# Group-norm roots taken on columns, and low weight parts formed by adding transfers, in a hybrid decoder layer

## The chip, the cores and the metric

The kernel runs on one core of a Trainium2 chip, with five engines that work side by side: TensorE (PE, with its weight loads as PEld), VectorE (DVE), ScalarE (ACT), GpSimd (POOL) and SyncE (SP, which only issues transfers). Sixteen DMA engines move data for all issuers. The metric is the device time of one execution in microseconds (us). Durations of single instructions are given in us or ns as the trace has them.

## The reference

One layer of a decoder trunk on a sequence of 1024 tokens with 1024 channels, in float32. A normalised input `hn` is projected once, and the projection is cut into the inputs of three mixers and their gates; the three branches are projected, gated and summed, and an MLP follows:

```
proj = hn @ w_in                                   # 1024 x 10256
ya = gmlp_mixer(za);  yb = rg_lru_mixer(zb);  yc = ssd_mixer(zc, xbc, dt_raw)
merged = sum_k sigmoid(gate_k) * (y_k @ w_branch_k)
h = h + merged @ w_out
h = h + relu(rms_norm(h) @ w_mlp_up)**2 @ w_mlp_down
out = rms_norm(h)
```

The change touches the last step of the SSD mixer and the weights of `w_in` and `w_branch_k`. The SSD mixer has four groups of 256 channels. Its output `y`, multiplied by silu(z), is normalised within each group, token by token:

```
yg = y.reshape(bsz, seq, 4, 256)
yg = yg * lax.rsqrt(jnp.mean(yg * yg, axis=-1, keepdims=True) + EPS)
y  = yg.reshape(bsz, seq, 1024) * norm_g
```

So one root is wanted for each token and group, 4096 in all.

## The kernel before

**Tiles and split operands.** Activations lie with channels on the 128 partitions and tokens along the free axis, in two halves of 512 tokens. A product in float32 is made from three products of a rounded type: each operand is split into a high part (a rounded copy) and a low part (the operand less its high part), and high x high, high x low and low x high are added in PSUM. `split` (L128 to L133) makes the pair: L132 copies on ACT, L133 subtracts on DVE or POOL.

**Units.** Most of the input projection runs as units (`one_unit`, L558): one unit makes 128 output channels of 1024 tokens, 48 matmuls of 512 columns at L554, and hands the PSUM tile `ps` to a `post` function. There are two `ps` buffers, so a unit may start once the post two units back has read its own. Its weights come from `wtile` (L521 to L529): a transfer issued by SP brings a 512 KB tile `raw` (two buffers), and the split makes `wh` and `wl` in a pool of six, which are three pairs. `ahead` keeps the weights of the present unit and of two more in the making: the pair of unit n+2 takes the buffers of unit n-1. Of every three tiles, two are subtracted on DVE and one on POOL. There are 74 such tiles: 50 of `w_in` in the first stage of the run, and 24 of the three `w_branch` matrices later. In each unit the first four matmuls use `wh` alone, the fifth is the first that reads `wl`.

**Side work.** After each unit the waiting generators do one step. For each SSD group (`ssd_stages`) the steps are `rows_in`, `s1_`, `s2_`, `s3_` and `s4_` for either half of the tokens. `rows_in` and `s2_` issue broadcasts from the DRAM scratch `acs_d` on POOL's queue (L662 to tiles `e`, L701 to tiles `h`). `s3_` multiplies the decayed terms (L728, L732 on PE, L735 to L738 on DVE) and squares the result (L740 on ACT, L741 on POOL). `s4_` takes the roots: a matmul with a tile of ones (L746) puts the sum over 128 channels into every partition, and a square root on ACT (L748), a reciprocal (L749) and four more operations on DVE (L750 to L753) make a tile of 128 x 512 roots, each partition holding the same row; L756 scales `z`, and L757 stores it. LRU units (`lru_units`) end in matmuls at L812, tanh and exp on ACT, a root on ACT (L824), products on POOL (L823, L826), and a scan on DVE (L827). `conv` (L574 to L577) reads a `ps` tile once on ACT (L575) and three times on DVE (L577). The four PSUM tiles `aux` are shared by all side work.

**What sets the order.** In this stage a scheduler puts the instructions of each engine in order by its own estimate of their times; the engines then run their queues strictly in that order, and a transfer's issue waits in its engine's queue for its data. The later stages (`with tc.manual_schedule()`) run in program order.

Of the kernel before, what the change touches and what calls it, by code (L numbers as in the profile page):

```python
# [8 lines left out]
F32 = mybir.dt.float32  # L9
F32R = mybir.dt.float32r  # L10
I32 = mybir.dt.int32
AF = mybir.ActivationFunctionType
ALU = mybir.AluOpType
# [3 lines left out]
P = 128  # L17
# [5 lines left out]
EPS = 1e-6  # L23
# [13 lines left out]
def trunk_kernel(ctx: ExitStack, tc: tile.TileContext, x, norm_mix_g, w_in, b_gate, gmlp_ln_g, gmlp_ln_b,  # L37
# [4 lines left out]
    nc = tc.nc  # L42
    x, w_in, b_gate, out = x[0], w_in[0], b_gate[0], out[0]
    w_out, w_up, w_dn = w_out[0], w_mlp_up[0], w_mlp_down[0]

    base = ctx.enter_context(tc.tile_pool(name="base", bufs=1))
# [28 lines left out]
    def half_(shape=(P, HF), dt=F32):  # L75
        return halfp.tile(list(shape), dt, tag="half", name=nm("h"))

    def aux():
        return auxp.tile([P, HF], F32, tag="aux", name=nm("aux"))
# [6 lines left out]
    tt = nc.vector.tensor_tensor  # L86
    stt = nc.vector.scalar_tensor_tensor
    ts = nc.vector.tensor_scalar
    actv = nc.scalar.activation
    mm = nc.tensor.matmul  # L90
# [37 lines left out]
    def split(dst_hi, dst_lo, src, eng=None, cast=None):  # L128
        if cast:
            cast.tensor_copy(out=dst_hi, in_=src)  # L130
        else:
            actv(dst_hi, src, AF.Copy)  # L132
        (eng or nc.vector).tensor_tensor(out=dst_lo, in0=src, in1=dst_hi.bitcast(F32), op=ALU.subtract)  # L133
# [151 lines left out]
    with tc.manual_schedule():  # L285
# [19 lines left out]
        ident = base.tile([P, P], F32, name="ident")  # L305
# [4 lines left out]
        nc.gpsimd.affine_select(out=tri, in_=ones, pattern=[[1, P]], compare_op=ALU.is_ge, fill=0.0,  # L310
                                base=0, channel_multiplier=-1)
        g2c = base.tile([P, 2 * KD], F32, name="g2c")
        eps4 = base.tile([P, 1], F32, name="eps4")
        nc.vector.memset(eps4, 4.0 * EPS)
        ss, rs = sm(NCH, "ss"), sm(NCH, "rsx")
        v2[NCH - 1] = act()

# [70 lines left out]
        for c in range(1, NCH):  # L388
# [5 lines left out]
            sq = gelu_in(c - 1)  # L394
# [123 lines left out]
            self.op["A22"] = [[t[:, 4 * p + kk, :] for kk in range(4)] for p in range(2)]  # L518


    def wtile(src, n=[0]):  # L521
        raw = rawp.tile([P, KD, P], F32, tag="raw", name=nm("raw"))
        nc.sync.dma_start(out=raw, in_=src.rearrange("(k p) e -> p k e", p=P))
        hi = wp.tile([P, KD, P], F32R, tag="w", name=nm("wh"))
        lo = wp.tile([P, KD, P], F32R, tag="w", name=nm("wl"))
        n[0] += 1
        split(hi, lo, raw, nc.gpsimd if n[0] % 3 == 0 else nc.vector)
        return hi, lo

    queue, ready, pending = [], [], []  # L530
# [118 lines left out]
    def ssd_stages(g, S):  # L649
# [5 lines left out]
        def tok(c):  # L655
            return slice(c * P, (c + 1) * P)
# [40 lines left out]
        def s2_(half):  # L697
            for j in range(2):
                t = er[half, j] = half_((P, 4, P))
                for h in range(2):  # L700
                    nc.gpsimd.dma_start(out=t[64 * h:64 * h + 64], in_=acs_v[1, half * 4:half * 4 + 4, 4 * g + 2 * j + h, :].partition_broadcast(64))  # L701
            for q in (2 * half, 2 * half + 1):
                if q == 0:
                    pv[0] = half_((P, 2, 256))
                    nc.gpsimd.memset(pv[0][:, 0, :], 0.0)
                st = aux()
                for cc in range(2):
                    mm(st[:, cc * 256:cc * 256 + 256], Bt[:, 2 * q + cc, :], xw[q][:, cc].rearrange("p h d -> p (h d)"), start=True, stop=True)
                for cc in range(2):
                    c = 2 * q + cc  # L710
                    if c == NCH - 1:
                        continue
                    if cc == 1:
                        pv[q + 1] = half_((P, 2, 256))
                    dst = pv[(c + 1) // 2][:, (c + 1) % 2, :]
                    for h in range(4):
                        col = c * 16 + 4 * g + h
                        o = slice(h * 64, h * 64 + 64)
                        stt(out=dst[:, o], in0=pv[q][:, cc, o], scalar=etot[:, col:col + 1],
                            in1=st[:, cc * 256 + h * 64:cc * 256 + h * 64 + 64], op0=ALU.mult, op1=ALU.add)  # L720

        def s3_(half):
# [17 lines left out]
                actv(sq[half, j], Z[:, tk], AF.Square)  # L740
            nc.gpsimd.tensor_tensor(out=sq[half, 0], in0=sq[half, 0], in1=sq[half, 1], op=ALU.add)  # L741

        def s4_(half):
            tk = hsl(half)
            vs = aux()
            mm(vs, ones, sq[half, 0], start=True, stop=True)  # L746
            r, q = half_(), half_()
            actv(r, vs, AF.Sqrt, scale=1.0 / 256, bias=eps4)  # L748
            nc.vector.reciprocal(out=r, in_=r)  # L749
            tt(out=q, in0=r, in1=r, op=ALU.mult)  # L750
            stt(out=q, in0=vs, scalar=256 * 4.0 * EPS, in1=q, op0=ALU.add, op1=ALU.mult)
            ts(out=q, in0=q, scalar1=-0.5 / 256, scalar2=1.5, op0=ALU.mult, op1=ALU.add)
            tt(out=r, in0=r, in1=q, op=ALU.mult)  # L753
            for j in range(2):
                Z = S["z", j]
                stt(out=Z[:, tk], in0=Z[:, tk], scalar=va[:, SNG + 2 * g + j:SNG + 2 * g + j + 1], in1=r, op0=ALU.mult, op1=ALU.mult)  # L756
                nc.gpsimd.dma_start(out=yd["c"][2 * g + j][:, tk], in_=Z[:, tk])  # L757

        rows_in(0)
# [6 lines left out]
        rows_in(1)  # L766
        yield
        s1_(1)
        s4_(0)
        yield  # L770
        s2_(1)
        yield
        s3_(1)
        yield
        yield
        s4_(1)


# [846 lines left out]
```

## Time and profile before

Three runs of the kernel took 2033.77, 2035.14 and 2036.89 us; the median is 2035.14 us. The profiled execution is a separate one, and its own time is 2038.13 us.

| | value |
|---|---|
| median of three runs | 2035.14 us |
| profiled execution, its own time | 2038.13 us |
| its span, first to last instruction | 2036.3 us |
| PE busy | 1968.3 us (97%) |
| DVE busy | 1286.2 us (63%) |
| ACT busy | 875.0 us (43%) |
| POOL busy | 328.1 us (16%) |
| mean granted TensorE clock | 0.986 of full speed |

Busy time is time in which an instruction of the engine ran; issues of transfers and waits on semaphores are not in it. PE's matmuls are pipelined and their ends are modelled, so the cost of a matmul is best read from start to start. A wait is put down to the producer that came last. The first stage with units and side work lies between 127 and 800 us, the products of the gates between 800 and 1030 us, the 24 branch units between 1030 and 1290 us.

### The profile page before, as it was taken

Reading aid. Unit: us, or ns where it says so; the run is one execution under the profiler, and the core shown is the slowest. Engines: PE = TensorE matmul, PEld = TensorE weight load, DVE = VectorE, ACT = ScalarE, POOL = GpSimd, SP = SyncE. Lnnn points to the kernel's source line nnn. Section 1 sums busy time; section 2 is a strip of 40 time slices with the busy share of each in tenths; the row PEclk is TensorE's granted clock in tenths of the full one; section 3 lists DMA queues with packets and bytes.
Section 4 is the critical chain, followed back from the end, with each engine's and each line's share of the span. In section 5 each row is a group of like instructions: output and inputs, shape, how many; then the busy total and the mean of one; then the engine's idle time right before and its main releaser. Section 6 shows DMA issues by size and latency. Waiting matters only on the chain.

```text
span 2036.3 us, 23707 instructions
## 1 busy us (share of the span) xinstructions
PE 1968.3 (97%) x9168; PEld 1639.5 (81%) x9168; DVE 1286.2 (63%) x1835; ACT 875.0 (43%) x1302; POOL 328.1 (16%) x362
## 2 busy tenths in 40 slices
PE   8999999999999999999999999999899999999996
PEld 7998878777778788788888888887688887888885
DVE  5596786874877787544452324336766557787787
ACT  6423554554546533444451111246555555253243
POOL 4012132231231343000000230000111111000000
PEclk8999999999999999999999999999999999999998
DMA  4223235224242343333393332421444438644532
GB/s 156 76 104 79 64 77 115 62 63 88 63 96 65 73 144 119 120 107 111 114 320 121 117 94 93 165 83 54 163 134 161 160 129 301 216 131 144 184 107 92
DMA packets 204517, 247.77 MB, mean 122 GB/s; under 512 B 11396, under 2 KB 148820, under 8 KB 204404
## 3 DMA queue, kind: packets, MB, share of 16 engines
q1 hardware_dynamic: 175636, 144.91, 23.9%
q0 software_dynamic: 22832, 79.84, 12.4%
q10 hardware_dynamic: 5936, 21.51, 3.0%
q8 instruction: 72, 1.18, 0.2%
q14 instruction: 41, 0.34, 0.1%
HBM read 178.97 MB, written 67.24 MB: 121 GB/s over the span
## 4 chain that ended last, share of the span: by engine, by line
PE 77%; DVE 10%; ACT 5%; DMA 4%; issue 2%; POOL 2%; SPq 0%; DVEq 0%; ACTq 0%; POOLq 0%
PE ps L554 31%; PE aux L478 30%; PE gps L478 6%; PE aux L257 4%; PE aux L1155 2%; DVE a L827 1%; DVE a L577 1%; DMA h<-acs_d 1%; PE aux L812 1%; DMA lr<-in_lru_w_i_dram 1%; DMA a<-in_x_dram 1%; ACT a L1196 1%; PE aux L856 1%; DVE rsq_q L111 1%; ACT a L132 1%
## 5 line engine op out<-in xcount | busy, mean ns | idle before, releaser
L554 PE MATMUL ps<-xn,wh 128*128 128x512 f32 x1600 | 440.5, 396 | 12.2 <-DVE a L577 12.2
L554 PEld LDWEIGHTS ps<-xn,wh 128*128 128x128 f32 x1600 | 301.4, 190 | 78.6 <-issue 12.7
L554 PE MATMUL ps<-xn,wl 128*128 128x512 f32 x800 | 248.9, 392 | 0.0
L478 PE MATMUL aux<-a,b 128*128 128x512 f32 x864 | 197.3, 389 | 0.0
L478 PEld LDWEIGHTS aux<-a,b 128*128 128x128 f32 x864 | 162.2, 188 | 33.6
L132 ACT ACTIVATE wh<-raw 128x1024 fp32r<-128x1024 f32 x74 | 78.0, 1055 | 255.8 <-PE ps L554 221.1
L554 PEld LDWEIGHTS ps<-xn,wl 128*128 128x128 f32 x800 | 151.7, 190 | 32.0
L478 PE MATMUL aux<-b,wt 128*128 128x512 f32 x672 | 156.9, 389 | 0.0
L478 PEld LDWEIGHTS aux<-b,wt 128*128 128x128 f32 x672 | 126.2, 188 | 26.1
L478 PE MATMUL aux<-b,b 128*128 128x512 f32 x480 | 110.6, 389 | 0.0
L1050 DVE SCALAR_TENSOR_TENSOR a<-a,ps 128x1024 f32<-128x1024 f32 x22 | 26.8, 1220 | 131.2 <-PE ps L554 86.3
L1377 DVE TENSOR_TENSOR a<-aux,a 128x512 f32<-128x512 f32 x112 | 77.1, 689 | 50.4 <-PE aux L478 50.4
L133 POOL TENSOR_TENSOR wl<-raw,wh 128x1024 fp32r<-128x1024 f32 x24 | 60.9, 2539 | 293.8 <-ACT wh L132 293.7
L133 DVE TENSOR_TENSOR wt<-a,wt 128x1024 fp32r<-128x1024 f32 x50 | 61.3, 1226 | 70.8 <-ACT wt L132 70.8
L478 PEld LDWEIGHTS aux<-b,b 128*128 128x128 f32 x480 | 90.1, 188 | 18.7
L133 DVE TENSOR_TENSOR wl<-raw,wh 128x1024 fp32r<-128x1024 f32 x50 | 66.2, 1325 | 45.9 <-ACT wh L132 38.6
L133 DVE TENSOR_TENSOR a<-a,a 128x1024 fp32r<-128x1024 f32 (+1 forms) x64 | 63.8, 1004 | 49.3 <-ACT a L132 49.2
L132 ACT ACTIVATE b<-wt 128x1024 fp32r<-128x1024 f32 x60 | 61.8, 1053 | 69.4 <-DMA wt<-u_d 65.0
L554 PE MATMUL ps<-c,wh 128*128 128x512 f32 x320 | 85.5, 389 | 0.0
L478 PE MATMUL aux<-a,wt 128*128 128x512 f32 x336 | 80.3, 396 | 3.3 <-ACT a L1254 3.3
L132 ACT ACTIVATE a<-a 128x1024 fp32r<-128x1024 f32 (+1 forms) x64 | 55.0, 879 | 56.4 <-DVE a L1329 45.2
L478 PEld LDWEIGHTS aux<-a,wt 128*128 128x128 f32 x336 | 64.1, 191 | 17.6 <-ACT a L1254 4.2
(336 smaller groups left out, 3699.5 us busy)
## 6 DMA issues: line engine op xcount, KB each, us to landing
wt<-u_d SPq DMA_DIRECT2D x54, 512.0 KB
raw<-in_w_in_dram SPq DMA_DIRECT2D x50, 512.0 KB
u_d<-a POOLq DMA_DIRECT2D x48, 512.0 KB, 5.1
g_d<-a POOLq DMA_DIRECT2D x24, 512.0 KB, 2.9
a<-g_d ACTq DMA_DIRECT2D x22, 512.0 KB
rt<-in_w_mlp_up_dram SPq DMA_DIRECT2D x17, 512.0 KB
a<-acs_d POOLq DMA_DIRECT2D x32, 256.0 KB, 8.1
a<-in_w_mlp_down_dram SPq DMA_DIRECT2D x16, 512.0 KB
```

What stands on the lines that cost most here:

```text
L111: stt(out=q, in0=r, scalar=nh, in1=r, op0=ALU.mult, op1=ALU.mult)
L132: actv(dst_hi, src, AF.Copy)
L133: (eng or nc.vector).tensor_tensor(out=dst_lo, in0=src, in1=dst_hi.bitcast(F32), op=ALU.subtract)
L257: mm(ps[:, :nt], X.tok(a, k, c), wk[k][w], start=(k == 0 and i == 0), stop=(k == KD - 1 and i == 2))
L478: mm(ps, lhs[l][kk], rhs[r][kk], start=(new and n == 0), stop=(n == 11), skip_group_check=not new)
L554: mm(ps[:, hsl(h)], w[wi][:, k, :], a.rhs(ai, k, h), start=(n == 0), stop=(n == 3 * KD - 1))
L577: stt(out=dst[:, j:], in0=ps[:, :T - j], scalar=taps[3 - j], in1=dst[:, j:], op0=ALU.mult, op1=ALU.add)
L812: mm(ps, w[wi][:, q * P:(q + 1) * P], S["xs"][half][ai], start=(n == 0), stop=(n == 2))
L827: nc.vector.tensor_tensor_scan(out=y[:, tk], data0=m, data1=ti, initial=(0.0 if half == 0 else y[:, HF - 1:HF]), op0=ALU.mult, op1=ALU.add)
L1050: stt(out=t, in0=t, scalar=1.0, in1=ps, op0=ALU.add, op1=ALU.mult)
L1155: mm(ps, M.tok(a, k, c), wo[nb][k][w], start=(k == 0 and a + w == 0), stop=(k == KD - 1 and a == 1))
L1377: tt(out=h, in0=ps, in1=h, op=ALU.add)
```

## The change

In `wtile` the low part is no longer subtracted by DVE or POOL. ACT copies `raw` to `wh`, then copies `wh` with factor -1 to `wl`, and POOL issues a transfer from `raw` to `wl` that adds to what lies there. In the SSD, `s4_` is cut in two. `roots_` sums squares with `sq` as the stationary operand and one column of ones as the moving one, 128 tokens at a time, so that the sums of 512 tokens land as four columns of 128; `rsqrt_cols` (three operations on DVE and twelve on POOL, all on 128 x 4 elements) makes the roots, in a tile `groot`. `s4_`, one step later, spreads each column of roots over all partitions by a matmul with the column, repeated 128 times, as stationary operand and the identity as moving one; L756 then reads the roots from PSUM. `rsqrt_cols` was there before, for the norm of the input rows.

```diff
@@ -310,8 +310,7 @@
         nc.gpsimd.affine_select(out=tri, in_=ones, pattern=[[1, P]], compare_op=ALU.is_ge, fill=0.0,
                                 base=0, channel_multiplier=-1)
         g2c = base.tile([P, 2 * KD], F32, name="g2c")
-        eps4 = base.tile([P, 1], F32, name="eps4")
-        nc.vector.memset(eps4, 4.0 * EPS)
+        groot = base.tile([P, 8], F32, name="groot")
         ss, rs = sm(NCH, "ss"), sm(NCH, "rsx")
         v2[NCH - 1] = act()
 
@@ -518,13 +517,14 @@
             self.op["A22"] = [[t[:, 4 * p + kk, :] for kk in range(4)] for p in range(2)]
 
 
-    def wtile(src, n=[0]):
+    def wtile(src):
         raw = rawp.tile([P, KD, P], F32, tag="raw", name=nm("raw"))
         nc.sync.dma_start(out=raw, in_=src.rearrange("(k p) e -> p k e", p=P))
         hi = wp.tile([P, KD, P], F32R, tag="w", name=nm("wh"))
         lo = wp.tile([P, KD, P], F32R, tag="w", name=nm("wl"))
-        n[0] += 1
-        split(hi, lo, raw, nc.gpsimd if n[0] % 3 == 0 else nc.vector)
+        actv(hi, raw, AF.Copy)
+        actv(lo, hi.bitcast(F32), AF.Copy, scale=-1.0)
+        nc.gpsimd.dma_start(out=lo, in_=raw, accum_op=ALU.add)
         return hi, lo
 
     queue, ready, pending = [], [], []
@@ -740,20 +740,20 @@
                 actv(sq[half, j], Z[:, tk], AF.Square)
             nc.gpsimd.tensor_tensor(out=sq[half, 0], in0=sq[half, 0], in1=sq[half, 1], op=ALU.add)
 
+        def roots_(half):
+            vs = aux()
+            for i in range(4):
+                mm(vs[:, i:i + 1], sq[half, 0][:, tok(i)], ones[:, :1], start=True, stop=True)
+            rsqrt_cols(groot[:, 4 * half:4 * half + 4], vs[:, :4], 1.0 / 256, 4.0 * EPS)
+
         def s4_(half):
             tk = hsl(half)
-            vs = aux()
-            mm(vs, ones, sq[half, 0], start=True, stop=True)
-            r, q = half_(), half_()
-            actv(r, vs, AF.Sqrt, scale=1.0 / 256, bias=eps4)
-            nc.vector.reciprocal(out=r, in_=r)
-            tt(out=q, in0=r, in1=r, op=ALU.mult)
-            stt(out=q, in0=vs, scalar=256 * 4.0 * EPS, in1=q, op0=ALU.add, op1=ALU.mult)
-            ts(out=q, in0=q, scalar1=-0.5 / 256, scalar2=1.5, op0=ALU.mult, op1=ALU.add)
-            tt(out=r, in0=r, in1=q, op=ALU.mult)
+            rb = aux()
+            for i in range(4):
+                mm(rb[:, tok(i)], groot[:, 4 * half + i:4 * half + i + 1].to_broadcast([P, P]), ident, start=True, stop=True)
             for j in range(2):
                 Z = S["z", j]
-                stt(out=Z[:, tk], in0=Z[:, tk], scalar=va[:, SNG + 2 * g + j:SNG + 2 * g + j + 1], in1=r, op0=ALU.mult, op1=ALU.mult)
+                stt(out=Z[:, tk], in0=Z[:, tk], scalar=va[:, SNG + 2 * g + j:SNG + 2 * g + j + 1], in1=rb, op0=ALU.mult, op1=ALU.mult)
                 nc.gpsimd.dma_start(out=yd["c"][2 * g + j][:, tk], in_=Z[:, tk])
 
         rows_in(0)
@@ -766,12 +766,15 @@
         rows_in(1)
         yield
         s1_(1)
-        s4_(0)
+        roots_(0)
         yield
         s2_(1)
+        s4_(0)
         yield
         s3_(1)
         yield
+        yield
+        roots_(1)
         yield
         s4_(1)
```

PE, in the first SSD group, the step of the second half of the tokens. `h_2186` and `h_2194` are the sums of squares of the first half, `lw` the weights of an LRU head, `ps_2396` and `ps_2415` the unit that runs then. Before:

```order
L682 MATMUL aux_2300<-a_1737,a_1647 128x128 x3
L746 MATMUL aux_2329<-h_2186,ones 128x512 [waits DVE_49,PE_49,Pool_49]
L812 MATMUL aux_2344<-h_2160,lw_2156 128x512 [waits Activation_49]
L812 MATMUL aux_2344<-h_2161,lw_2156 128x512
L812 MATMUL aux_2344<-h_2160,lw_2157 128x512
L554 MATMUL ps_2396<-xn_224,wh_2095 128x512
```

and after, in the same place:

```order
L682 MATMUL aux_2309<-a_1740,a_1649 128x128 x3
L746 MATMUL aux_2338<-ones,h_2194 128x1 [waits DVE_49,PE_49,Pool_49]
L746 MATMUL aux_2338<-ones,h_2194 128x1 x3
L554 MATMUL ps_2415<-xn_223,wh_2102 128x512 [waits Activation_49]
L554 MATMUL ps_2415<-xn_536,wh_2102 128x512
```

PE after, one unit further on, where the spread stands:

```order
L708 MATMUL aux_2490<-h_2291,a_1890 128x256 [waits DVE_49]
L708 MATMUL aux_2490<-h_2291,a_1890 128x256
L708 MATMUL aux_2502<-h_2300,a_1890 128x256 [waits Activation_49]
L708 MATMUL aux_2502<-h_2300,a_1890 128x256
L753 MATMUL aux_2509<-ident,groot 128x128 [waits Activation_49,Pool_49]
L753 MATMUL aux_2509<-ident,groot 128x128 x3
L554 MATMUL ps_2525<-xn_223,wh_2225 128x512
```

One matmul of 512 columns has become four of one column, and four of 128 columns stand behind the unit and ahead of the next one; `aux_2509` is the tile of spread roots.

POOL, at the same place. `wl` is a low part, `h_2465` and `h_2484` are tiles of the second half that the broadcast at L701 fills, `yb_d` and `yc_d` the stores of an LRU head and of the SSD. Before:

```order
L826 TENSOR_TENSOR h_2376<-h_2376,h_2370 128x512 [waits Activation_49]
L133 TENSOR_TENSOR wl_2493<-raw_2490,wh_2492 128x1024 [waits DMAHW2_49,PE_49,Activation_49]
L829 TENSOR_TENSOR a_2270<-a_2343,a_2270 128x1024 [waits DVE_49]
L830 DMA yb_d<-a_2270 128x1024 [waits Pool_49]
L701 DMA h_2465<-acs_d 64x4x128
L701 DMA h_2465<-acs_d 64x4x128 [waits DMASW1_49]
L701 DMA h_2468<-acs_d 64x4x128 [waits DMASW2_49,PE_49]
L701 DMA h_2468<-acs_d 64x4x128 [waits DMASW3_49]
```

and after:

```order
L829 TENSOR_TENSOR h_2372<-h_2372,h_2366 128x512 [waits Activation_49]
L829 TENSOR_TENSOR h_2394<-h_2394,h_2388 128x512 [waits Activation_49]
L832 TENSOR_TENSOR a_2279<-a_2361,a_2279 128x1024 [waits DVE_49]
L833 DMA yb_d<-a_2279 128x1024 [waits Pool_49]
L527 DMA wl_2521<-raw_2518 128x1024 [waits DMASW1_49,DMAHW2_49,PE_49,Activation_49]
L757 DMA yc_d<-a_1953 128x512 [waits DMASW2_49,DVE_49]
L757 DMA yc_d<-a_2065 128x512 [waits DMASW3_49,DVE_49]
L701 DMA h_2484<-acs_d 64x4x128 [waits DMASW4_49]
L701 DMA h_2484<-acs_d 64x4x128 [waits DMASW5_49]
L701 DMA h_2487<-acs_d 64x4x128 [waits DMASW6_49]
L701 DMA h_2487<-acs_d 64x4x128 [waits DMASW7_49]
```

The two stores of `yc_d`, which stood ahead of the LRU's products (L823, L826) and so ahead of the first of these rows, now stand between the adding transfer and the four broadcasts, so that the broadcasts issue behind both.

ACT, in the second SSD group, where the units of x and z end. `wh` is the high part of a later unit, L575 the read of a finished `ps`, `lw` the weights of an LRU head, `a_2906` and `a_2957` the tiles `e`. Before:

```order
L132 ACTIVATE wh_2914<-raw_2912 128x1024 [waits DMAHW7_49,PE_49]
L575 ACTIVATE a_2897<-ps_2848,vh,scw 128x1024 [waits PE_49]
L627 ACTIVATE a_2902<-a_2897 128x1024 [waits DVE_49,Activation_49]
L132 ACTIVATE lw_3176<-lr_3173 128x256 [waits DMAHW3_49,DMAHW2_49]
L691 ACTIVATE a_2906<-a_2906,acs 128x128 [waits DMASW7_49]
L691 ACTIVATE a_2906<-a_2906,acs 128x128 x3
L691 ACTIVATE a_2906<-a_2906,acs 128x128 [waits DMASW0_49]
L691 ACTIVATE a_2906<-a_2906,acs 128x128 x3
```

and after, in the same place:

```order
L525 ACTIVATE wh_2965<-raw_2963 128x1024 [waits DMAHW7_49,PE_49]
L575 ACTIVATE a_2948<-ps_2899,vh,scw 128x1024 [waits PE_49]
L526 ACTIVATE wl_2966<-wh_2965 128x1024 [waits DMASW2_49,Activation_49]
L627 ACTIVATE a_2953<-a_2948 128x1024 [waits DVE_49,Activation_49]
L691 ACTIVATE a_2957<-a_2957,acs 128x128 [waits DMASW0_49]
L691 ACTIVATE a_2957<-a_2957,acs 128x128 x3
L691 ACTIVATE a_2957<-a_2957,acs 128x128 [waits DMASW1_49]
```

ACT after, further on, where `lw` stands:

```order
L691 ACTIVATE a_2960<-a_2960,acs 128x128 x3
L525 ACTIVATE wh_3077<-raw_3075 128x1024 [waits DMAHW0_49]
L692 ACTIVATE a_2960<-a_2960 128x1024 [waits Activation_49]
L526 ACTIVATE wl_3078<-wh_3077 128x1024 [waits Activation_49]
L132 ACTIVATE lw_3230<-lr_3227 128x256 [waits DMAHW3_49,DMAHW2_49]
```

The copy to `wl` stands behind L575 in every unit, and the copy `lw`, which stood ahead of the first L691, now stands behind the last L692.

## Rows read from the trace of the kernel before

**Rows 1.** The page, first part: the span, and busy time, share and instruction count of two engines.

```profile
span 2036.3 us, 23707 instructions
...
PE 1968.3 (97%) x9168; PEld 1639.5 (81%) x9168; DVE 1286.2 (63%) x1835; ACT 875.0 (43%) x1302; POOL 328.1 (16%) x362
```

**Rows 2.** Stretches of 50 us of the first stage: length, busy us (instructions) of PE, PEld, DVE, ACT and POOL, granted clock of PE, share of the DMA engines, GB/s.

```profile
250.00:300.00 50.00, 46.59 (x225) 37.21 (x223) 40.17 (x43) 26.47 (x30) 19.04 (x15) 0.97 0.29 74
...
450.00:500.00 50.00, 46.45 (x237) 38.21 (x236) 25.97 (x42) 21.54 (x42) 11.91 (x15) 0.97 0.47 100
500.00:550.00 50.00, 48.11 (x245) 39.70 (x243) 39.66 (x55) 27.17 (x38) 14.83 (x14) 0.97 0.25 63
...
650.00:700.00 50.00, 45.50 (x215) 36.94 (x214) 40.73 (x55) 24.30 (x32) 15.75 (x15) 0.93 0.31 74
```

**Rows 3.** PE's waits over the whole run: the waiting line, whom it waited for, us in total, times, longest.

```profile
PE ps L554 <- DVE a L577: 12.2, 8, 2.6
...
PE aux L812 <- DVE h L735: 3.9, 4, 1.9
PE aux L708 <- ACT a L678: 3.5, 1, 3.5
...
PE aux L728 <- DVE h L719: 2.1, 1, 2.1
```

**Rows 4.** PE's timeline around one of these waits: start, us, line, operands, count; in brackets the idle time before it and its cause.

```profile
252.56 1.07 PE L554 MATMUL ps<-xn,wh 128*128 128x512 f32 x4
...
258.18 2.05 PE L554 MATMUL ps<-xn,wh 128*128 128x512 f32 x4 [2.63 <-DVE a L577]
```

**Rows 5.** Groups of instructions by line and shape: count, busy us, mean ns, idle time before.

```profile
L132 ACT ACTIVATE wh<-raw 128x1024 fp32r<-128x1024 f32 x74 | 78.0, 1055 | 255.8 <-PE ps L554 221.1 <-issue 23.7 <-DMA raw<-in_w_branch_c_dram 9.2
...
L133 DVE TENSOR_TENSOR wl<-raw,wh 128x1024 fp32r<-128x1024 f32 x50 | 66.2, 1325 | 45.9 <-ACT wh L132 38.6 <-PE aux L728 7.2
...
L133 POOL TENSOR_TENSOR wl<-raw,wh 128x1024 fp32r<-128x1024 f32 x24 | 60.9, 2539 | 293.8 <-ACT wh L132 293.7
...
L749 DVE RECIPROCAL h<-h 128x512 f32<-128x512 f32 x8 | 26.8, 3347 | 2.2 <-ACT h L748 2.2
```

**Rows 6.** DVE's timeline through one chain of roots (from its reciprocal to the scaling at L756) and the next `conv`.

```profile
372.02 3.35 DVE L749 RECIPROCAL h<-h 128x512 f32<-128x512 f32 x1
...
378.05 1.42 DVE L756 SCALAR_TENSOR_TENSOR a<-a,va,h 128x512 f32<-128x512 f32 x2
...
390.80 3.91 DVE L577 SCALAR_TENSOR_TENSOR a<-ps,va,a 128x1023 f32<-128x1023 f32 x3
```

**Rows 7.** PE's timeline at one sum of squares (L746), with the 128-column matmuls ahead of it (L682) and what follows; below, all weight loads of L746: min, median and max ns.

```profile
225.93 1.06 PE L682 MATMUL aux<-a,a 128*128 128x128 f32 x8
...
226.82 1.02 PE L746 MATMUL aux<-h,ones 128*128 128x512 f32 x2
...
227.28 1.26 PE L812 MATMUL aux<-h,lw 128*128 128x512 f32 x3
...
228.38 0.84 PE L554 MATMUL ps<-xn,wh 128*128 128x512 f32 x3
...
L746 PEld LDWEIGHTS aux<-h,ones x16: 188/190/192, 226.7 to 713.5; 128*128 128x128 f32 x16
```

**Rows 8.** POOL's small root operations as they run for the input rows: min, median and max ns.

```profile
L123 POOL TENSOR_TENSOR rsqn_q<-rsqn_r x9: 192/193/420, 11.5 to 39.2; 128x3 f32<-128x3 f32 x6, 128x1 f32<-128x1 f32 x3
```

**Rows 9.** Transfers: the software queue's packets, MB and share of 16 engines' span; then issues by line with KB of each and median us from issue to landing, the last line within 440 to 480 us alone.

```profile
q0 software_dynamic: 22832, 79.84, 12.4%
...
u_d<-a POOLq DMA_DIRECT2D x48, 512.0 KB, 5.1
g_d<-a POOLq DMA_DIRECT2D x24, 512.0 KB, 2.9
...
a<-vn_d POOLq DMA_DIRECT2D x8, 512.0 KB, 7.0
...
a<-acs_d POOLq DMA_DIRECT2D x8, 256.0 KB, 10.6
```

**Rows 10.** The start of the branch units: SP's issue of two weight loads, ACT's first high part from them, the first matmuls of the first and second unit, and a stretch of 10 us (columns as in rows 2).

```profile
1021.87 2.87 SPq L523 DMA_DIRECT2D raw<-in_w_branch_c_dram  x2
...
1032.95 1.06 ACT L132 ACTIVATE wh<-raw 128x1024 fp32r<-128x1024 f32 x1 [1.43 <-DMA raw<-in_w_branch_c_dram]
...
1030.03 1.07 PE L554 MATMUL ps<-a,wh 128*128 128x512 f32 x4
...
1040.91 1.07 PE L554 MATMUL ps<-a,wh 128*128 128x512 f32 x4
...
1030.00:1040.00 10.00, 10.00 (x45) 8.26 (x44) 6.27 (x6) 6.25 (x7) 0.53 (x1) 1.00 1.06 383
```

**Rows 11.** A broadcast at L701 on POOL, the first user of its data on DVE, and PE's matmuls of the same step, by start.

```profile
394.03 2.48 POOL L701 DMA_DIRECT2D h<-acs_d  x4
...
402.10 0.69 DVE L735 TENSOR_TENSOR h<-aux,h 128x512 f32<-128x512 f32 x1 [1.27 <-DMA h<-acs_d]
...
402.94 0.93 PE L812 MATMUL aux<-h,lw 128*128 128x512 f32 x3 [0.35 <-DVE h L735]
```

**Rows 12.** ACT's copy of an LRU weight and the PE step that follows, by start.

```profile
472.69 0.42 ACT L132 ACTIVATE lw<-lr 128x256 fp32r<-128x256 f32 x1 [14.62 <-DMA lr<-in_lru_w_i_dram]
...
478.13 2.90 PE L708 MATMUL aux<-h,a 128*128 128x256 f32 x8 [3.55 <-ACT a L678]
```

## The prediction

> **What bounds the kernel now.** I read the page's busy shares first: PE works 97% of the span [rows 1], so the gain can be no more than PE's idle time, its time at a lower clock, and matmuls removed. The stretches of 50 us come next [rows 2]; the reader is to see that PE is short of 50 busy us where the granted clock is also under 1.00, so that a wait costs more than its own length. PE's waits by line then say who causes them [rows 3]: `ps` waiting for the last DVE operation of `conv` (8 times, 12.2 us), L812 for L735 (3.9 us), one wait of 3.5 us at L708, one of 2.1 us at L728. PE's timeline at one of the conv waits shows what follows [rows 4]: four matmuls after an idle stretch of 2.63 us take 2.05 us, where the same four took 1.07 us before it; PE is back at the lower of its two levels (1.2 instead of 2.4 GHz) for a while. So this is a kernel bound by PE, with some 22 us of small waits in the stage that the change touches, and DVE behind most of them.
>
> **Weights: what goes.** 50 subtractions of 1.325 us leave DVE, 66.2 us, and 24 of 2.54 us leave POOL, 60.9 us [rows 5]. **Roots: what goes.** On DVE the chain from reciprocal to scaling runs from 372.02 to 378.05 us, 6.03 us [rows 6]; its reciprocal alone is 3.35 us, eight times 26.8 us [rows 5]. Eight chains are 48 us. DVE so falls from 1286 to about 1172 us, plus three tiny operations a half.
>
> **(a) Conv waits.** A `conv` keeps DVE 3.91 us [rows 6], and PE waits 1.5 us in the mean, 2.6 at most [rows 3]. One subtraction less ahead of a conv brings it 1.3 us forward, a chain less 6 us; nearly each wait should shrink or go. The idle time is 12.2 us; the clock lost in three stretches is 50 x (0.03 + 0.03 + 0.07) = 6.5 us [rows 2] (the stretch from 450 us belongs to (c)). Together 18.7 us. Some of these convs are late for another reason (L575 on ACT, or two convs in a row), so I take three quarters: -14 us; bounds 0 and -18.7.
>
> **(b) L728 on L719**: a DVE operation again, -2 us (bounds 0 and -2.1).
>
> **(c) The LRU weight.** At 472.69 us ACT had waited 14.62 us for the transfer of `lr`, and with it the copies L691 and L692 that stood behind; PE then lost 3.55 us at L708 [rows 12] and 50 x 0.03 = 1.5 us of clock [rows 2]. The changed order has `lw` behind the last L692, so that ACT does the SSD's work first. 5.05 us are to be had; the LRU's own matmuls may come later for it, so I take -4 us (bounds 0 and -5).
>
> **(d) Roots on PE.** One sum over 512 columns (two passes) goes, eight instructions of 128 columns for the spread come. From 226.82 to 228.38 us stand the sum and three matmuls of 512 columns [rows 7]; a unit's 48 take 1040.91 - 1030.03 = 10.88 us, 0.227 us each [rows 10], so the sum itself cost 1.56 - 0.68 = 0.88 us. The spread: eight times the pitch of L682, 0.89 us for eight [rows 7], is 0.89 us. These two are even. What remains are the eight instructions of one column, each with a weight load of 128 columns. Nothing like it is in the trace. At the pitch of L682 they are 0.86 us a half, 6.9 us in eight; if a weight load's whole latency of 190 ns showed [rows 7], 64 x 0.19 = 12.2 us; if the loads ran beside the matmuls before them, near 0. I take the row that it is nearest to, +6.9 us. The twelve operations on POOL (192 ns for one like them [rows 8], some 3.6 us with gaps, an estimate) and three on DVE lie beside the unit of 10.9 us that now stands between `roots_` and `s4_`; without that cover PE would wait some 4 us for each of eight halves.
>
> **(e) Broadcasts L701.** POOL's queue is strictly in order, and an adding transfer waits there for ACT's second copy. Behind it now stand the two stores of `yc_d`, which wait for L756 behind the spread, and behind these the four broadcasts of the second half. Before, they were issued from 394.03 us, 2.48 us for four; L735 still waited 1.27 us for their data, and L812 0.35 us for L735 [rows 11]. By the new order I expect the issue within some microseconds of the old, some halves earlier (POOL no longer subtracts for 2.54 us ahead of them), some later. If all came early, the 3.9 us of [rows 3] would go; if each of four came 3 us late, +12. I take +2 us.
>
> **(f) Low parts that arrive by transfer.** ACT gets 74 copies of 1.055 us [rows 5], 78 us, going from 43% [rows 1] to about 47%; they stand behind L575, so no `ps` is released later, and I cost them at nothing (a copy that did hold a release would cost its 1.055 us). POOL's issue takes 0.62 us [rows 11]. How long an adding transfer T takes no row shows. Plain ones of 512 KB land in 2.9 us (`g_d`), 5.1 (`u_d`) and 7.0 (`vn_d`) [rows 9], and in a crowded stretch in 11.1 (1021.87 to 1032.95 us, DMA share 1.06) [rows 10]. In the first stage the share is 0.25 to 0.47 [rows 2], a pair is made two units of 10.9 us ahead, and 5 to 7 us hide. The buffers of `raw` give the limit: there are two, so load (7.0 us, the slowest quiet row), copies and issue (1.06 + 1.06 + 0.62 = 2.7 us) and T must fit into two units, 21.8 us: T up to about 12 us costs nothing. At the start of the branch units less is at hand: the high part starts at 1032.95 us, the copies end at 1035.1, the add is issued by 1035.7, and the second unit, from 1040.91 us, wants the low part after four matmuls, at 1041.8 [rows 10]. 6.1 us are left: none lost at T = 5.1, 5.0 us at T = 11.1. I take +2 us (bounds 0 and +12, for two such stalls and the clock behind them).
>
> The Trainium skill ("Collectives: The Full Stack", section "The bandwidth ceiling: the fold count and why AG ≠ RS ≠ AR") holds that a reducing transfer is slow not because of the addition but because "the add needs **two source reads**" on one ring, and so moves at half the rate. By the software queue, 79.84 MB took 12.4% of 2036.3 us [rows 9, 1], so 512 KB keep all sixteen engines for 1.66 us, and an add would by that rule keep them 3.3 us. Hidden in the first stage, it would bring the branch start some 3.3 us more of stall, and the sum below to -4.8 us instead of -8.1. No row here shows an adding transfer, so the rule is left out of the sum.
>
> **(g) Broadcasts to `e`** (L662, 10.6 us to land in a crowded stretch [rows 9]) also stand behind adds; one issue of 0.62 us more ahead of each of eight is 5 us at most, +1 us taken.
>
> **Sum**: -14 - 2 - 4 + 6.9 + 2 + 2 + 1 = -8.1 us. The profiled execution took 2038.13 us (its span 2036.3 and 1.8 around it), so 2030.0; it is 3.0 us over the median of the runs, so 2027.0 us as a median. Own range 2016 to 2036.
>
> **Rivals.**
> *More gain.* All of (a), (b), (c) goes and half of (d) is hidden beside matmuls: -18.7 - 2.1 - 5 + 3.4 = -22.4, 2012.7 us. For it: DVE has 114 us less and was behind most waits. Against: a queue that is freed tends to wait for the next in line. Chance 0.14.
> *No change.* PE pays the latency of 64 weight loads in full (+12.2), and only half of the conv time comes back (-9.4): -9.4 - 2 - 4 + 12.2 + 2 + 2 + 1 = +1.8, 2036.9 us. For it: the 190 ns of [rows 7] and a small column count to hide them. Against: L682's pitch of 0.11 us with the same loads. Chance 0.18.
> *Slower: POOL's queue.* Each add holds POOL until ACT has made both copies and the `wl` buffer is free; broadcasts L701 and root operations stand behind. If in each of eight halves L735 comes 2 us later than PE can bear, that is 2 us idle and about 1 us of clock [rows 4], 24 us instead of the 2 of (e): +13.9, 2049 us. It decides from broadcasts landing more than about 1 us later than now, as L735 is late already [rows 11]. Against: POOL is busy 16% [rows 1]. Chance 0.14.
> *Slower: the ring.* T of 16 us would make two units last 4 us longer than 21.8; over 12 pairs of branch units with clock some 54 us, 2081 us. Decides from T = 12. Against: no quiet plain transfer is over 7 us; for it: 11.1 us where it is crowded. Chance 0.08.
> *It doesn't do what it says*: DVE is not behind the conv waits, but ACT or the order; little changes. Chance 0.02.
>
> **Numbers.** My forecast has 0.44. About 0.2%, 4 us, can be told from no change. Faster: 0.35 of the forecast's chance, 0.14 and 0.03 of the no-change case, 0.52; within: 0.09 + 0.11 + 0.02 = 0.22; slower: 0.04 + 0.14 + 0.08 = 0.26. The range 2010 to 2052 us takes in the first three rivals and leaves out the ring and the tails.
>
> **What will show it.** (a): no conv row, or one under 4 us, among PE's waits, and stretches at 1.00. (c): L708's wait gone. (d): pitch of the eight one-column matmuls, 0.11 or 0.19 us, and no wait of L753 on POOL. (e): L735's wait for `acs_d`, and L812's for L735. (f): median landing of the adds, 5 to 7 us, and PE's waits for `wl` at L554 near 1042 us. I am wrong if PE waits for `wl` all along, or if new waits on POOL add up to more than 10 us.

## The result, and the profile after

The changed kernel took 2040.22 us (median of 20 runs) against 2035.84 us before (20 runs): ratio 1.0025, interval 1.0016 to 1.0033. It became slower by 0.2%, where the prediction had 2027 us and faster. The profiled execution took 2037.77 us, at the lower end of its runs (2037.65 to 2044.23).

The page, first part, as in [rows 1]:

```profile
span 2036.1 us, 24175 instructions
...
PE 1973.0 (97%) x9280; PEld 1649.8 (81%) x9280; DVE 1166.0 (57%) x1768; ACT 917.6 (45%) x1348; POOL 354.4 (17%) x508
```

DVE has 120 us less (114 were worked out), and the span is the same: PE waits 4.9 us less (span less busy time) and is busy 4.7 us longer. Its waits, as in [rows 3]:

```profile
PE aux L815 <- DVE h L735: 13.4, 4, 3.8
...
PE aux L600 <- DVE adt L595: 1.7, 1, 1.7
PE ps L554 <- DMA wl<-raw: 1.3, 1, 1.3
...
PE aux L815 <- DVE h L736: 0.9, 2, 0.7
```

The conv waits (12.2 us), L728 for L719 and L708 are gone, all of them. In their place the LRU's matmuls (L815, which was L812) wait for L735, four times 2.9 to 3.8 us, once in each SSD group. The granted clock followed the waits to their new places, as the stretches of [rows 2] show:

```profile
250.00:300.00 50.00, 46.25 (x231) 37.86 (x230) 29.80 (x41) 24.88 (x29) 16.72 (x28) 0.97 0.52 113
...
450.00:500.00 50.00, 50.00 (x262) 41.89 (x261) 25.83 (x44) 28.01 (x54) 10.78 (x17) 1.00 0.71 143
500.00:550.00 50.00, 46.45 (x240) 38.44 (x239) 32.48 (x54) 24.92 (x32) 18.56 (x28) 0.93 0.46 99
...
650.00:700.00 50.00, 46.72 (x228) 37.95 (x227) 32.51 (x54) 26.68 (x36) 20.52 (x31) 0.93 0.48 106
```

For the second SSD group, the same step by start on three engines (POOL's issues, DVE's first user of their data, PE), which answers to [rows 11]:

```profile
388.89 0.91 POOL L527 DMA_DIRECT2D wl<-raw  x1
389.44 1.49 POOL L757 DMA_DIRECT2D yc_d<-a  x2
390.77 2.65 POOL L701 DMA_DIRECT2D h<-acs_d  x4
```

```profile
402.14 0.69 DVE L735 TENSOR_TENSOR h<-aux,h 128x512 f32<-128x512 f32 x1 [7.45 <-DMA h<-acs_d]
```

```profile
394.98 1.05 PE L728 MATMUL aux<-a,h 128*128 128x128 f32 x8
...
402.98 4.79 PE L815 MATMUL aux<-h,lw 128*128 128x512 f32 x12 [3.82 <-DVE h L735]
407.61 1.07 PE L554 MATMUL ps<-xn,wh 128*128 128x512 f32 x4
```

The broadcasts were issued 3.3 us earlier than before (390.77 against 394.03 us), and their data came at the same time, 402.1 us. What had changed is on either side of them: an adding transfer and two stores now stand just ahead of them in the software queue, and PE came to the step sooner, since nothing had held it. PE then waited 3.82 us, and its twelve matmuls took 4.6 us, from 402.98 to 407.61, at the lower clock.

Transfers of the changed kernel, then of the kernel before (median us from issue to landing last):

```profile
wl<-raw POOLq DMA_DIRECT2D x74, 512.0 KB, 5.3
...
h<-acs_d POOLq DMA_DIRECT2D x32, 128.0 KB, 11.5
```

```profile
h<-acs_d POOLq DMA_DIRECT2D x32, 128.0 KB, 8.8
```

At the start of the branch units the second unit found no low part:

```profile
1036.62 0.73 PE L554 MATMUL ps<-c,wh 128*128 128x512 f32 x2 [0.53 <-DVE c L133]
...
1039.03 1.07 PE L554 MATMUL ps<-a,wh 128*128 128x512 f32 x4
1041.36 0.74 PE L554 MATMUL ps<-a,wl 128*128 128x512 f32 x2 [1.26 <-DMA wl<-raw]
```

PE began these units 2.9 us earlier than before (1027.2 against 1030.0 us) and began the last matmuls of the same tiles at the same 1283.7 us. Two lengths serve below: the *first stage*, from the first to the last start of a matmul `ps<-xn,wh`, and the *branch stretch*, likewise for `ps<-a,wh`. Before, then after (length, PE's busy us first, clock third from the end):

```profile
127.40:815.10 687.70, 664.86 (x3251) 548.66 (x3251) 513.01 (x668) 323.45 (x463) 189.30 (x185) 0.99 0.35 86
...
1030.00:1283.70 253.70, 253.70 (x1121) 210.13 (x1120) 91.64 (x80) 52.60 (x57) 40.88 (x16) 1.00 0.42 138
```

```profile
126.90:813.90 687.00, 670.87 (x3365) 560.56 (x3364) 421.14 (x634) 339.08 (x483) 218.77 (x314) 0.99 0.54 123
...
1027.20:1283.70 256.50, 254.70 (x1121) 209.76 (x1120) 69.22 (x64) 76.98 (x80) 39.11 (x32) 1.00 0.68 186
```

### The profile page after: what moved, and what is told of

The parts are those of the page before. It is cut to its first block, busy times and chain, and to the rows that moved or that the text cites. A ratio compares the mean times of both kernels' runs of the same rounds, so it can differ in the third digit from the quotient of the medians.

```text
span 2036.1 us, 24175 instructions
## 1 busy us (share of the span) xinstructions
PE 1973.0 (97%) x9280; PEld 1649.8 (81%) x9280; DVE 1166.0 (57%) x1768; ACT 917.6 (45%) x1348; POOL 354.4 (17%) x508
## 4 chain that ended last, share of the span: by engine, by line
PE 77%; DVE 10%; DMA 4%; ACT 4%; POOL 3%; issue 2%; SPq 0%; DVEq 0%; POOLq 0%; ACTq 0%
PE ps L554 33%; PE aux L477 30%; PE gps L477 5%; PE aux L257 3%; DMA h<-acs_d 2%; PE aux L1158 2%; PE aux L815 1%; DVE rsq_q L111 1%; ACT a L1199 1%; PE aux L859 1%; DVE a L830 1%; DMA raw<-in_w_branch_c_dram 1%; DMA wl<-raw 1%; ACT a L132 1%; DVE a L133 1%
## 5 line engine op out<-in xcount | busy, mean ns | idle before, releaser
L554 PE MATMUL ps<-xn,wh 128*128 128x512 f32 x1600 | 434.4, 392 | 0.0
L527 POOL DMA_DIRECT2D wl<-raw x74 | 66.0, 891 | 403.9 <-ACT wl L526 292.3
L132 ACT ACTIVATE b<-wt 128x1024 fp32r<-128x1024 f32 x60 | 61.8, 1053 | 70.1 <-DMA wt<-u_d 51.2
L132 ACT ACTIVATE a<-a 128x1024 fp32r<-128x1024 f32 (+1 forms) x64 | 55.1, 879 | 56.5 <-DVE a L1332 43.8
L526 ACT ACTIVATE wl<-wh 128x1024 fp32r<-128x1024 f32 x74 | 77.8, 1052 | 0.8
```

The lines of the kernel that those rows point to most:

```text
L526: actv(lo, hi.bitcast(F32), AF.Copy, scale=-1.0)
L527: nc.gpsimd.dma_start(out=lo, in_=raw, accum_op=ALU.add)
L554: mm(ps[:, hsl(h)], w[wi][:, k, :], a.rhs(ai, k, h), start=(n == 0), stop=(n == 3 * KD - 1))
```

## The experiments

Theory P: the loss is the late broadcasts L701 of the second half. Rivals: M, the loss is the one-column matmuls on PE; Q, PE is only early, and some next producer would hold it anyway. The table has each run's median, its ratio to the kernel before on the same chip, and the two lengths, in us; each length is that of the one traced execution of the run:

| run | median | ratio (interval) | first stage | branch stretch |
|---|---|---|---|---|
| before | 2035.84 | | 687.7 | 253.7 |
| after | 2040.22 | 1.0025 (1.0016 to 1.0033) | 687.0 | 256.5 |
| x1_after | 2042.17 | 1.0040 (1.0026 to 1.0055) | 690.0 | 259.7 |
| x2_roots | 2031.72 | 0.9988 (0.9977 to 0.9998) | 680.7 | 253.7 |
| x3_adds | 2031.84 | 0.9990 (0.9982 to 0.9999) | 681.6 | 258.9 |
| x4_sp | 2039.70 | 1.0028 (1.0017 to 1.0039) | 687.0 | 259.8 |
| y1_early | 2016.81 | 0.9915 (0.9900 to 0.9931) | 662.7 | 256.8 |
| y2_bsplit | 2036.13 | 1.0010 (0.9997 to 1.0024) | 684.1 | 253.6 |
| y3_both | 2011.89 | 0.9890 (0.9873 to 0.9908) | 662.6 | 253.6 |
| y4_rearly | 2013.24 | 0.9897 (0.9881 to 0.9914) | 661.9 | 253.7 |
| y5_bearly | 2029.35 | 0.9970 (0.9958 to 0.9982) | 677.5 | 253.6 |
| z1_adearly | 2022.83 | 0.9934 (0.9921 to 0.9947) | 671.1 | 258.0 |
| z2_twice | 2016.81 | 0.9906 (0.9892 to 0.9920) | 669.8 | 253.6 |
| z3_plain | 2011.93 | 0.9882 (0.9868 to 0.9897) | 660.7 | 254.3 |
| w1_plain | 2025.47 | 0.9950 (0.9937 to 0.9963) | 672.7 | 255.7 |
| w2_ycsp | 2025.60 | 0.9954 (0.9941 to 0.9967) | 674.9 | 259.7 |

**The change again, and its two parts alone.** x1_after is the changed kernel; x2_roots has the `wtile` of before; x3_adds has the `s4_` of before.

> The changed kernel once more, unchanged, for a second trace. If the four waits of L815 for L735 (13.4 us in the first trace, against 3.9 at the same step before) and the stall at the start of the branch units (PE 2.9 us ahead at 1027 us, level again at 1284 us) are what the change costs, both come back within 2 us each. If they were an accident of one execution, L815's waits lie anywhere between 4 and 13 us. Ratio 1.000 to 1.004.

> Only the roots on columns; low parts are subtracted on DVE and POOL as before. Theory P (broadcasts L701 land late because the adding transfers stand ahead of them in the software queue): they are issued behind yc_d still, but land in about 9 us instead of 11.5; L815's waits at 4 to 8 us, and some of the conv waits go with the root chains: about 2033 us, ratio 0.997 to 1.000. Theory M (the one-column matmuls eat what DVE gives back): most of the loss is here already, ratio 1.001 to 1.004.

> Only the adding transfers; roots on 512 columns as before, so the yc_d stores and the broadcasts L701 stand in the old order. Theory P: L701 lands in 11 us or more here too, with L812 waiting 6 to 14 us for L735, and the branch start loses 2 to 3 us; conv waits go for half: ratio 1.000 to 1.003. Theory M: without the one-column matmuls 5 to 8 us are gained, ratio 0.996 to 0.998.

The second trace has the same four waits (16.3 us) and a longer branch stretch (259.7 us), so both costs are real; they came back 2.9 and 3.2 us larger, more than the 2 us expected, so they vary from one execution to another. Each part alone *gains* 2.5 us, so theory M and a theory that blames one part fall; together they lose. Both expectations were off in part: in x2_roots the waits for L734 are 11.4 us instead of 4 to 8, and in x3_adds the broadcasts landed in 9.1 us, not in 11 or more, while the branch stretch lost 5.2 us. Neither part alone has a conv wait left; of x2_roots (L734 is L735, L814 is L815), then of x3_adds (L736, L813):

```profile
PE aux L814 <- DVE h L734: 11.4, 7, 5.3
```

```profile
PE aux L813 <- DVE h L736: 11.7, 5, 3.5
...
PE aux L729 <- DVE h L720: 2.6, 4, 0.7
```

Either part takes enough off DVE to end the conv waits, so the second brings no more of that, but its own price comes on top; and either way PE runs into the broadcasts.

**Broadcasts by SP.**

```diff
-                    nc.gpsimd.dma_start(out=t[64 * h:64 * h + 64], in_=acs_v[1, half * 4:half * 4 + 4, 4 * g + 2 * j + h, :].partition_broadcast(64))
+                    nc.sync.dma_start(out=t[64 * h:64 * h + 64], in_=acs_v[1, half * 4:half * 4 + 4, 4 * g + 2 * j + h, :].partition_broadcast(64))
```

> The changed kernel with the 32 broadcasts L701 issued by SP instead of POOL, so that they stand behind neither the adds nor the yc_d stores. Theory P: they land in 5 to 9 us, L815's wait for L735 falls from 13 us under 4 us, and 8 to 13 us come back against the changed kernel: ratio 0.995 to 0.999 against the kernel before. Theory M: 0 to 3 us come back, ratio 1.001 to 1.003.

The expectation of theory P was missed: L815 still waited 12.5 us for L735. The trace shows why the run doesn't decide: the broadcasts stood in SP's queue behind a load of `raw` that was issued some 22 us after the load ahead of it, when its buffer came free, and so they were issued at 253.96 us in the first group, 3 us later than by POOL.

**Broadcasts one step earlier.** y1_early on the changed kernel, y4_rearly on the roots alone, y5_bearly on the kernel before, z1_adearly on the adds alone:

```diff
         rows_in(1)
         yield
+        er_(1)
         s1_(1)
...
-        def s2_(half):
+        def er_(half):
             for j in range(2):
                 t = er[half, j] = half_((P, 4, P))
...
+        def s2_(half):
+            if half == 0:
+                er_(0)
```

> The changed kernel with the four broadcasts L701 of the second half issued one step earlier, with s1_ instead of s2_, so that they stand ahead of the roots, of an adding transfer and of the yc_d stores. Theory P (PE waits in the second half's step for broadcasts that land late): L735's wait for acs_d falls from 29 us to under 6, L815's wait for L735 from 13 to 16 us to under 4, the first stage gets 8 to 13 us shorter than 687 to 690 us, ratio 0.997 to 1.000. Theory Q (PE is simply there too early, and the next producer in line holds it): L815's or another wait of the same step stays at 8 us or more, and under 4 us come back, ratio 1.001 to 1.004.

> Only the roots on columns, no adding transfer anywhere, and the broadcasts one step earlier. Theory P: the 11.4 us of waits for L734 that the roots alone showed fall under 4 us, and the time is 8 to 12 us under that of the roots alone (2031.7): ratio 0.992 to 0.996. Theory Q: the waits stay at 8 us, ratio 0.997 to 1.000.

> The kernel before, with nothing of the change, and only the broadcasts L701 of the second half one step earlier. Theory P: before the change these broadcasts cost little (L812 waited 3.9 us for L735), so 4 to 8 us are gained and the conv waits of 12 us stay: ratio 0.996 to 0.998. Theory R (the early broadcast is worth some 20 us in any kernel, and the change itself nothing): ratio 0.988 to 0.992.

> Only the adding transfers, roots on 512 columns as before, with the broadcasts one step earlier. Theory P: the waits for L736 of 11.7 us go, the first stage falls from 681.6 to 665 to 670 us, the branch stretch stays at 256 to 260 us: ratio 0.990 to 0.994. If DVE's long root chains hold PE here, a conv or L720 wait of over 5 us is left and the ratio is 0.995 to 0.998.

Theory P held, with twice the gain expected: 23 to 25 us by the medians, 24.3 us in the first stage (and y4_rearly 18.5 us under the roots alone). In y1_early neither L735 nor L815 waits for a transfer, and what is left of PE's waits in that stage is 1.8 us; the step that took 12.6 us from L728 to the next unit takes 7.0 (L732 and L820 are L728 and L815):

```profile
PE aux L600 <- DVE adt L595: 1.8, 1, 1.8
```

```profile
388.12 1.05 PE L732 MATMUL aux<-a,h 128*128 128x128 f32 x8
...
392.24 3.02 PE L820 MATMUL aux<-h,lw 128*128 128x512 f32 x12
...
395.09 1.07 PE L554 MATMUL ps<-xn,wh 128*128 128x512 f32 x4
```

```profile
125.50:788.20 662.70, 660.95 (x3364) 555.55 (x3364) 421.31 (x634) 339.52 (x483) 218.38 (x314) 1.00 0.55 128
```

Of the 24.3 us, 14.4 were idle time (687.0 - 670.9 against 662.7 - 661.0) and 9.9 busy time. The LRU's 96 matmuls behind the waits alone are 8.5 of these (33.4 us busy against 24.9): the twelve from 402.98 us ran at a mean granted clock of 0.63, those of y1_early at 1.00. My expectation had priced the idle time alone. Q falls: no other producer stepped in. On the kernel before, the same edit brought only 7 us (10.2 in the first stage), and waits for conv stayed:

```profile
PE ps L554 <- DVE a L577: 8.6, 4, 2.6
PE aux L732 <- DVE h L723: 5.7, 4, 2.7
PE aux L712 <- ACT a L678: 1.7, 1, 1.7
```

So theory R, that the early broadcast is worth the same in any kernel, falls too: against the kernel before, the early broadcast alone is worth 6.8 us, the change alone costs 4.4 or more, and together they gain some 17 (ratio 0.9915). z1_adearly gained 9 us on x3_adds, and no wait for the broadcasts was left. With DVE's long root chains still there it kept 7.9 us of waits for L724 (before, L719), and its first stage, 671.1 us, stayed 8 to 9 us over that of y1_early and y4_rearly, so both halves of its expectation came in part.

**The branch units.** y2_bsplit subtracts the low parts of the 24 branch tiles as before; y3_both adds the early broadcasts.

```diff
+        n[0] += 1
+        if n[0] > 50:
+            split(hi, lo, raw, nc.gpsimd if n[0] % 3 == 0 else nc.vector)
+            return hi, lo
```

> The changed kernel with the low parts of the 24 branch tiles subtracted on DVE and POOL as before; adding transfers for the 50 tiles of w_in alone. If the adds cost 3 to 6 us at the start of the branch units (256.5 to 259.8 us from the first to the last unit there, against 253.7 before), the stretch is 253.7 us again, no wait for wl is left, and the time falls by 3 to 6 us: ratio 1.000 to 1.002. If the stall is the crowded transfers in any case, it stays over 256 us and the ratio at 1.002 to 1.004.

> Both of these edits on the changed kernel. If the two places are all that the change costs and are separate, the gains add: 11 to 18 us under the changed kernel, ratio 0.994 to 0.998. If they share a cause (the software queue as such), the sum is under 8 us, ratio 0.998 to 1.000.

The branch stretch is as before, with no wait for `wl`, in both. The gains add, 28 us under the changed kernel, some 10 more than the top of the expectation for the reason given. y3_both is faster than either kernel, 1.1% under the kernel before.

**The price of the one-column matmuls.** On y3_both:

```diff
                 mm(vs[:, i:i + 1], sq[half, 0][:, tok(i)], ones[:, :1], start=True, stop=True)
+                mm(vs[:, 8 + i:9 + i], sq[half, 0][:, tok(i)], ones[:, :1], start=True, stop=True)
```

> The kernel of y3_both with every one-column matmul of roots_ done twice (the second set into columns that nothing reads). If they cost PE their pitch of 0.10 us in full, 64 more take 6.5 us: the first stage 669 us against 662.6, the time about 2018. If they lie beside other work, under 2 us, 2012 to 2014.

The median grew by 4.9 us, on another chip than that of y3_both (by the ratios some 3 us, with intervals that overlap). The first stage grew by 7.2 us, all of it busy time of PE, so they cost PE their pitch; sixteen instructions from 226.96 to 228.67 us:

```profile
226.96 0.28 PE L754 MATMUL aux<-ones,h 128*128 128x1 f32 x2
...
228.67 0.94 PE L558 MATMUL ps<-xn,wh 128*128 128x512 f32 x3
```

**The price of adding in a transfer, and what makes the broadcasts late.** In z3_plain (on y1_early) and w1_plain (on the changed kernel, its order untouched) each adding transfer is a plain one of the same tiles: the addition is left out, so the low part holds the whole weight. In w2_ycsp the `yc_d` stores are issued by SP.

```diff
-        nc.gpsimd.dma_start(out=lo, in_=raw, accum_op=ALU.add)
+        nc.gpsimd.dma_start(out=lo, in_=raw)
```

> The kernel of y1_early with the adding transfer replaced by a plain one of the same tiles (the low part then holds the whole weight, so the addition is left out). If the add costs by its second read, the plain transfer lands in 3 us or so against 5.2, the software queue's share falls from 22.9% to 18 to 20%, and the branch stretch is 253.7 to 255 us against 256.8: 2013 to 2016. If an add costs no more than a plain transfer, all three stay, 2016 to 2018.

> The changed kernel, its order untouched, with each adding transfer replaced by a plain one of the same tiles (the addition is left out). It tells whether the broadcasts L701 come late because the adds ahead of them in the software queue are slow, or because they are issued late. If the slow adds: L701 lands in 8 to 9 us as without adds (11.5 now), L815's waits fall from 13 to 16 us to 5 to 9, and with the 2 to 5 us at the branch start 10 to 15 us come back, 2025 to 2030. If the place of the issue: L815 still waits 11 us or more and only the branch start's part comes back, 2033 to 2038.

> The changed kernel with the sixteen yc_d stores issued by SP, so that the four broadcasts stand in POOL's queue right behind the adding transfer and wait for no spread of roots. If the stores ahead of them make them late: L701 is issued some 2 us earlier (at about 249.6 instead of 250.9 us in the first group) and lands without the stores' 1 MB ahead of it, L815's waits fall under 8 us, 2022 to 2032. If the add alone does: they stay at 11 us or more, 2036 to 2042.

The software queue and the transfer of z3_plain, then of y1_early:

```profile
q0 software_dynamic: 33488, 118.64, 18.3%
...
wl<-raw POOLq DMA_DIRECT2D x74, 512.0 KB, 3.4
```

```profile
q0 software_dynamic: 33488, 118.64, 22.9%
...
wl<-raw POOLq DMA_DIRECT2D x74, 512.0 KB, 5.2
```

An add lands 1.8 us later than a plain transfer. On the changed kernel, w1_plain got 14.8 us back and w2_ycsp 14.6, of some 25; L815's waits, w1_plain first:

```profile
PE aux L815 <- DVE h L735: 4.9, 7, 1.5
PE aux L815 <- DVE h L736: 3.7, 8, 0.7
```

```profile
PE aux L815 <- DVE h L736: 3.5, 7, 0.7
PE aux L815 <- DVE h L735: 3.3, 2, 3.0
```

In both, PE's waits shrink, all but one to 1.5 us or less, and with them the matmuls at the lower clock: the slow add and the two stores each bear a part. From the first issue to L735's first start the four groups took 10.4 to 11.4 us in the changed kernel, and 7.9 to 9.2 us in w1_plain and w2_ycsp, but for one of 11.9 us. (The two stores of a step are 0.5 MB, not the 1 MB of the expectation.) The landing is not the whole of it: in x2_roots and x3_adds it took 6.3 to 9.8 us, and PE still waited over 11 us, since there POOL issued later, at 253.47 and 256.59 us in the first group against 250.90; in x2_roots a subtraction of 2.4 us and the two stores ran on POOL just ahead. What is left of w1_plain's first stage over z3_plain's, 12 us, is the place of the issue, the one edit between the two.

## Why the prediction was wrong

**The bound, and (a), (b), (c): right.** PE was held by DVE's lateness, and all these waits went. They may even have been worth more than the -20 us taken: y4_rearly's first stage, 661.9 us, has almost no wait; without the 7 us of (d) that leaves some 655 us (an estimate) as what PE needs of its own in the kernel before, so 33 us were lost there, of which the early broadcast (y5_bearly) took 10 and (a) to (c) are most of the rest, some 23. With the broadcasts early in both kernels, the change takes 14.8 us off the first stage (677.5 to 662.7) with (d) in it, which makes some 22.

**(d): right.** +6.9 us taken (by its own row, 0.89 us for eight [rows 7], the term was 7.1); the doubled matmuls cost 7.2 in the first stage. The spread waited for nothing on POOL: no such wait of L753 is in the trace, and POOL's twelve operations ran beside the unit.

**(e): the step that failed.** "By the new order I expect the issue within some microseconds of the old" was right (3.3 us earlier, even), but I took +2 us from the issue alone. Two things were left out. The landing was not that of before: 11.5 us in the median against 8.8, behind an add and two stores. And PE would be there sooner, by the very gain of (a), while L735 already was late [rows 11]. The early broadcast gives back 24.3 us of the first stage after the change and 10.2 before it, so the term was +14 us, above its own bound of 12: that bound had no clock in it, and 9.9 of the 24.3 us are clock. This was the rival on POOL's queue, with the place right (L735, L815) and the cause partly: ahead of these broadcasts POOL did not wait for ACT (no idle time stands before the add at 388.89 us, nor in the other three groups); their data came late behind the add and the stores.

**(f): mechanism right, size off.** The stall came at the unit that was named, and the stretch lost 2.8 us in the first trace and 6.0 in the second, against +2; y2_bsplit and y3_both show it at 253.6 us. Here too PE came earlier, by 2.9 us, while ACT's first copy started only 0.7 us earlier (1032.21 against 1032.95 us), so less than the 6.1 us of the prediction was at hand. Not all of the loss is a wait for an add: in both traces the first unit waited 0.5 us for a low part of the activations `c`, in the second 1.1 us more for a high part (L132), whose copies stand behind ACT's two copies of a weight tile. (f) had put these copies at nothing. w1_plain, without adds, kept both waits (0.5 and 1.0 us) and a stretch of 255.7 us. How the loss divides between the adds and the copies stays open. The waits of the second trace there:

```profile
PE ps L554 <- DMA wl<-raw: 1.9, 1, 1.9
...
PE ps L554 <- ACT c L132: 1.1, 1, 1.1
```

Adds landed in 5.3 us in the median, and PE waited for no other `wl`, so the ring of `raw` did not bind. (g) showed no cost.

With -22 to -23 for (a) to (c), +7, +14 and +3 to +6, the sum is +1 to +5 us; the prediction's was -8.1. 2040.22 us lies over the forecast's own range (2016 to 2036) and within the wide one only because rivals had widened it. The rival of no change came nearest (2036.9 us), but by luck alone: the conv waits went in full and the one-column matmuls cost 7 us, not 12.2. The two traces differ by 9.6 us of span, 3.0 of it in the first stage and 3.2 in the branch stretch, and the medians over the runs are +4.4 and +7.8 us. So some 3 us of the larger figure are in no term, and what makes the same waits longer in one execution than in another stays open.

## What to carry to other kernels

When a change takes waits away, every transfer whose data the freed engine wants next must come sooner by as much; read its margin (issue, landing, first use) from the profile before, and move its issue in the same edit. Two edits that remove the same wait do not add, but their prices do: try each alone. And price a wait of some microseconds on PE with the slower matmuls behind it: here 14.4 us idle brought 9.9 us more.

## What was not expected of the hardware

An adding transfer kept the DMA engines nearly twice as long as a plain one of the same tile. With adds the software queue's packets took 22.9% of 16 x 2014.5 us, with plain transfers 18.3% of 16 x 2009.0, with neither (y4_rearly) 12.7% of 16 x 2012.3: the differences, divided by 74, are 44 and 24 us of one engine's time for 512 KB, a ratio of 1.8. The Trainium skill ("Collectives: The Full Stack", section "The bandwidth ceiling: the fold count and why AG ≠ RS ≠ AR") says of the reduce step of ring collectives that it is slow for its two source reads, at half the rate. The 1.8 of this trace, for a transfer within one core, is near that factor; the reads themselves no trace here shows. The prediction had left the rule out of its sum.

The issue of an adding transfer also took POOL longer, 0.88 us in the median against 0.54 for a plain one (w1_plain), and the issue of the broadcasts behind them took 794 ns in the median of the changed kernel, against 652 in w1_plain and 628 before.
